# A LoRA linear layer on one core: chunk 2 loaded in 48 and 16 rows, and the drains of three engines put elsewhere or left out

## The chip, the core and the metric

The kernel runs on one core of a Trainium2 chip. The metric is device time in microseconds (us) of one execution, less is better. Before the change the median of 15 runs is 161.18 us (161.04 to 161.37). The profile is of one further execution of 161.05 us.

## The reference

```python
x_flat = x.reshape(-1, in_dim)            # 32768 x 256, float32
y = x_flat @ W                            # W: 256 x 256
lora_out = ((x_flat @ lora_A) * lora_E) @ lora_B    # rank 16
return (y + scale * lora_out).reshape(batch, seq_len, out_dim)   # float32
```

The input x is 33.55 MB and the output as much; the weights are small.

## The kernel before, in words

The low-rank part is folded into one matrix at the start (`weff` = W + A·E·B·scale, L229 to L246 on VectorE and L285 to L291 on TensorE), so that each row of x is multiplied once.

**Chunks, rows and homes.** The 32768 rows are cut into four chunks of 8.39 MB. A chunk lies in SBUF as 128 partitions of 64 rows of 1 KB, so that a partition's part of a chunk is 64 KB, contiguous in HBM. There are three homes for four chunks (`home(c)`, c modulo 3): chunk 3 is loaded into chunk 0's home after chunk 0 has been stored. The result of each row overwrites the row in its home.

**The queue.** One list, ORDER (L18 to L33), gives the order of the transfers that SyncE (SP) issues: ("L", c, s, e) loads rows s to e of each partition of chunk c (L156), and ("S", c, s, e) stores them (L161). A DMA of r rows makes one packet of r KB for each partition, 128 packets in all. A load of chunk 3 waits for the stores of chunk 0 that cover its rows (L155), a store waits for the rows to be computed (L160, `s_done`). All six loads of chunks 0 to 2 are issued at the start, one behind the other. The first store, ("S", 0, 0, 40), is queued behind them.

**The groups.** A chunk is 16 groups of 4 rows. For each of the 64 groups GpSimd (POOL) casts the rows to bfloat16 (`stage`, L200), TensorE transposes them (L258), VectorE copies the transposed words out of PSUM (`xt`, L242), TensorE multiplies by `weff` (L269) and ScalarE (ACT) copies the result home (L221).

**The hold.** At the first group of chunk 2, named HELD (L39), GpSimd waits until the first store has landed (HOLDERS, L40, the wait in `gpsimd_program`), and so do all engines behind it.

**The drains.** `drain(engine, n)` (L170 to L175) waits on its engine for the load that begins at HELD and then issues n drain instructions that do nothing else. It is called at HELD by GpSimd (10), ScalarE (22) and VectorE (12); the counts stand in L44 to L46. The instructions lengthen the engine's program, which is fetched from HBM by DMAs of its own, in packets of 8192 bytes on queue 14.

**The ends of chunk 2.** SP stores rows 2 to 62 of chunk 2. Its first two and last two rows are stored by GpSimd in three DMAs (`share`, L164 to L168) over the partition ranges in SHARES (L37): 108 to 113, 0 to 108, 113 to 128. Each makes packets of 4096 bytes on queue 0.

Of the kernel before, what the change touches and what calls it, by code (L numbers as in the profile page):

```python
# [21 lines left out]
    ("L", 0, 40, 64),  # L22
    ("L", 1, 0, 32),
    ("L", 1, 32, 64),
    ("L", 2, 0, 64),
    ("S", 0, 0, 40),
    ("S", 0, 40, 64),
    ("L", 3, 0, 32),
# [10 lines left out]
HELD = (2, 0)  # L39
# [1 line left out]

WARM_UP = 2

VECTOR_DRAINS = 12  # L44
GPSIMD_DRAINS = 10
SCALAR_DRAINS = 22  # L46

CG = 4
GPC = ROWS // CG
# [8 lines left out]
def kernel(  # L58
# [37 lines left out]
    loaded = {op: sem(f"loaded_{op[1]}_{op[2]}") for op in ORDER if op[0] == "L"}  # L96
# [22 lines left out]
    def home(c):  # L119
        return homes[c % N_HOMES]  # L120

    sync, gpsimd, scalar, vector, tensor = nc.sync, nc.gpsimd, nc.scalar, nc.vector, nc.tensor
# [41 lines left out]
    def share(engine, p, landed):  # L164
        def ends_of(rows):
            return rows[p].rearrange("p (q b) k -> p q b k", b=END_ROWS)[:, :: ROWS // END_ROWS - 1, :, :]

        engine.dma_start(out=ends_of(y_chunks[SHARED]), in_=ends_of(home(SHARED))).then_inc(landed, 16)  # L168

    def drain(engine, n):  # L170
        for op, landed in loaded.items():
            if op[1:3] == HELD:
                engine.wait_ge(landed, 16)
        for _ in range(n):
            engine.drain()  # L175

    def gpsimd_program():
        gpsimd.memset(ident[:], 0.0).then_inc(s_ident, 1)  # L178
        gpsimd.wait_ge(s_ident, 1)
        gpsimd.affine_select(  # L180
            out=ident[:],
            in_=ident[:],
            compare_op=ALU.not_equal,
            fill=1.0,
            base=0,
            pattern=[[-1, P]],
            channel_multiplier=1,
        ).then_inc(s_ident, 1)
        for g in range(N_GROUPS):
            c, b = g // GPC, g % GPC * CG  # L190
            for op, landed in loaded.items():
                if op[1:3] == (c, b):
                    gpsimd.wait_ge(landed, 16)
            if (c, b) == HELD:
                drain(gpsimd, GPSIMD_DRAINS)
                for op in HOLDERS:
                    gpsimd.wait_ge(stored[op], 16)
            if g >= NS:
                gpsimd.wait_ge(s_turned, g - NS + 1)
            gpsimd.tensor_copy(out=stage[g % NS][:], in_=home(c)[:, b:b + CG, :]).then_inc(s_stage[g % UNROLL], 1)  # L200

        gpsimd.wait_ge(s_turned, N_GROUPS - NS + 1)
        gpsimd.drain().then_inc(s_stage[N_GROUPS % UNROLL], 1)
        gpsimd.wait_ge(s_shared, 1)
        for p in SHARES:
            share(gpsimd, p, shared_stored)

    def scalar_program():
        for name, to, of in (
            ("w", w_sb, W.rearrange("(q t) m -> q t m", t=KT)),  # L210
            ("b", b_sb, lora_B),
            ("e", e_sb, lora_E[:, None]),
        ):
            ins = scalar.dma_start(out=to[:], in_=of).then_inc(set_up_loaded[name], 16)
            opening.append(ins.ins.name)
        for g in range(N_GROUPS):
            c, b = g // GPC, g % GPC * CG
            if (c, b) == HELD:
                drain(scalar, SCALAR_DRAINS)
            scalar.wait_ge(s_y, g + 1)  # L220
            scalar.copy(out=home(c)[:, b:b + CG, :], in_=psum_y[g % NY][:]).then_inc(s_free[(g + NY) % UNROLL], 1)  # L221
            if (c, b + CG) == (SHARED, ROWS):
                scalar.drain().then_inc(s_shared, 1)
            if g in ends:
                scalar.drain().then_inc(s_done, 1)  # L225

    def vector_program():
        vector.wait_ge(set_up_loaded["e"], 16)
        vector.wait_ge(s_pe_set_up, 1)  # L229
        vector.tensor_scalar(  # L230
            out=ate[:],
            in0=psum_y[0][:R, :KT, :P],
            scalar1=e_sb[:],
            scalar2=float(scale),
            op0=ALU.mult,
            op1=ALU.mult,
        ).then_inc(s_ate, 1)
        for g in range(N_GROUPS):
            if (g // GPC, g % GPC * CG) == HELD:
                drain(vector, VECTOR_DRAINS)  # L240
            vector.wait_ge(s_turned, g + 1)
            vector.tensor_copy(out=xt[g % NX][:], in_=psum_xt[g % NT][:].bitcast(BF16)).then_inc(s_xt[g % UNROLL], 1)  # L242
            if g == 0:
                vector.wait_ge(set_up_loaded["w"], 16)
                vector.wait_ge(s_pe_set_up, 2)
                vector.tensor_add(out=weff[:], in0=w_sb[:], in1=psum_y[1][:, :KT, :]).then_inc(s_free[0], 1)  # L246
                vector.drain().then_inc(s_free[1], 1)

    def tensor_program():
        def turn(i, result=None):  # L250
# [53 lines left out]
    with tc.tile_critical(no_gpsimd_drain=True):  # L304
        sync_program()
        gpsimd_program()
        scalar_program()
        vector_program()
        tensor_program()
# [35 lines left out]
```

## Time and profile before

| What | Value |
|---|---|
| median of 15 runs | 161.18 us |
| the profiled execution, its own time | 161.05 us |
| its span, first to last instruction | 159.70 us |
| busy: PE, POOL, ACT, DVE | 95.1, 69.3, 66.1, 45.4 us |
| moved by DMA | 67.43 MB, mean 422 GB/s over the span |
| queue 1 (SP's loads and stores) | 2016 packets, 66.60 MB |
| queue 0 (GpSimd's stores) | 224 packets, 0.52 MB |
| queue 14 (instructions), in the span | 3 packets, 0.02 MB |
| loads of chunks 0 to 2 issued | 0.43 to 4.37 us |
| first store issued, landed | 28.68, 74.91 us |
| last store issued | 122.97 us |

The page of the profile gives busy time by engine, the span in 40 slices with the DMA rate in each, the DMA queues, the chain of waits that ended last, and groups of instructions by line. Windows of the span can be asked for: each gives the busy time of the engines, the granted TensorE clock (PEclk), the mean busy share of the 16 DMA engines, and the rate in GB/s; a window counts a packet where it starts.

Beneath these views the trace records every DMA packet with its start, its duration, its queue and its size. The record does not name the DMA engine, but the packets follow each other end to start within a few ns and so join into exactly 16 sequences, called lanes here, one for each DMA engine. In the middle of a run of equal packets a packet of 64 KB takes 2.418 us, one of 40 KB 1.514, of 32 KB 1.213, of 24 KB 0.912, of 16 KB 0.611, and an instruction packet 0.309 us.

### The profile page before, as it was taken

What the parts mean: (1) busy time and instruction counts of PE and PEld (TensorE: products, weight loads), DVE (VectorE), ACT (ScalarE), POOL (GpSimd) and SP (SyncE); (2) the same over time, 40 slices, a digit from 0 to 9 for tenths busy, and PEclk for the clock granted to TensorE, in tenths of its full rate; (3) what the DMA queues carried; (4) which work ended last, traced back from release to release, by engine and by line L of the source; (5) the groups of instructions that cost most, each with busy time, mean ns of one, the idle gap of its engine ahead of it and who ended that gap; (6) DMA issues with size and microseconds to landing.
All of it is one profiled execution on the core that took longest, in us unless ns stands there. A gap on an engine that the chain in (4) does not pass through costs nothing.

```text
span 159.7 us, 2070 instructions
## 1 busy us (share of the span) xinstructions
PE 95.1 (60%) x782; PEld 83.8 (52%) x782; DVE 45.4 (28%) x66; ACT 66.1 (41%) x65; POOL 69.3 (43%) x73
## 2 busy tenths in 40 slices
PE   2669999999999700000999999999995000000000
PEld 1146999999999600000789999999994000000000
DVE  0113555555555400000155555555551000000000
ACT  3001677777777700000257777777776000000000
POOL 1072777777777100002577777777763000000000
PEclk9965999999999995555589999999999655555555
DMA  7999999999979897989999999999989998979986
GB/s 271 427 443 443 400 453 427 484 402 394 591 328 525 361 427 328 466 359 441 412 476 412 419 468 419 533 394 394 509 371 400 482 454 352 529 327 498 425 380 263
DMA packets 2451, 67.43 MB, mean 422 GB/s; under 512 B 512, under 2 KB 528, under 8 KB 784
## 3 DMA queue, kind: packets, MB, share of 16 engines
q1 hardware_dynamic: 2016, 66.60, 97.5%
q0 software_dynamic: 224, 0.52, 0.9%
q10 hardware_dynamic: 208, 0.28, 0.6%
q14 instruction: 3, 0.02, 0.0%
HBM read 33.85 MB, written 33.55 MB: 422 GB/s over the span
## 4 chain that ended last, share of the span: by engine, by line
PE 40%; DMA 34%; POOL 1%; ACT 1%; issue 0%; SPq 0%; ACTq 0%
DMA out_dram<-home 29%; PE psum_y L269 25%; PE psum_xt L258 14%; DMA home<-in_x_dram 5%; POOL stage L200 1%; ACT home L221 1%; PE psum_y L291 1%; SPq L147 0%; ACTq L225 0%
## 5 line engine op out<-in xcount | busy, mean ns | idle before, releaser
L200 POOL CAST stage<-home 128x1024 bf16<-128x1024 f32 x64 | 66.5, 1042 | 48.8 <-DMA out_dram<-home 22.3
L221 ACT COPY home<-psum_y 128x1024 f32<-128x1024 f32 x64 | 64.8, 1013 | 54.8 <-PE psum_y L269 54.8
L269 PE MATMUL psum_y<-weff,xt 128*128 128x256 bf16 x512 | 68.7, 279 | 0.0
L242 DVE COPY xt<-psum_xt 128x1024 bf16<-128x1024 bf16 x64 | 44.3, 692 | 67.0 <-PE psum_xt L258 67.0
L258 PE MATMUL psum_xt<-ident,stage 128*128 128x128 f32 x260 | 41.6, 284 | 23.9 <-POOL stage L200 23.9
L269 PEld LDWEIGHTS psum_y<-weff,xt 128*128 128x128 bf16 x512 | 51.4, 100 | 6.2
L258 PEld LDWEIGHTS psum_xt<-ident,stage 128*128 128x128 f32 x260 | 31.9, 147 | 26.3 <-issue 25.1
L282 PE MATMUL psum_y<-ident 128*128 128x512 f32 x4 | 3.4, 1006 | 2.9 <-POOL ident L180 2.9
L282 PEld LDWEIGHTS psum_y<-ident 128*128 128x128 f32 x4 | 1.2, 323 | 3.9 <-POOL ident L180 2.9
L168 POOL DMA_DIRECT2D out_dram<-home x3 | 2.0, 676 | 1.0 <-PE psum_xt L258 1.0
L230 DVE TENSOR_SCALAR ate<-psum_y,e_sb 16x256 f32<-16x256 f32 x1 | 0.5, 472 | 6.6 <-DMA e_sb<-in_lora_E_dram 6.6
L221 ACT ACT_TABLE_LOAD x1 | 1.3, 1283 | 2.0 <-SPq L304 2.0
L291 PE MATMUL psum_y<-b_sb,ate 16*128 16x256 f32 x4 | 2.1, 670 | 0.0
L291 PEld LDWEIGHTS psum_y<-b_sb,ate 16*128 16x128 f32 x4 | 1.2, 319 | 0.5 <-issue 0.3
L246 DVE TENSOR_TENSOR weff<-w_sb,psum_y 128x512 bf16<-128x512 f32 x1 | 0.7, 687 | 1.4 <-PE psum_y L291 1.4
L178 POOL MEMSET ident<- 128x128 f32 x1 | 0.2, 205 | 1.7 <-SPq L304 1.7
L285 PEld LDWEIGHTS psum_y<-ident,a_sb 128*16 128x16 f32 x2 | 0.2, 114 | 0.9 <-issue 0.9
L180 POOL TENSOR_SCALAR_AFFINE_SELECT ident<-ident 128x128 f32<-128x128 f32 x1 | 0.3, 284 | 0.2 <-POOL ident L178 0.2
L285 PE MATMUL psum_y<-ident,a_sb 128*16 128x128 f32 x2 | 0.4, 273 | 0.0
L326 POOL MEMSET const-float32-0.0<- 128x1 f32 x1 | 0.1, 93 | 0.2 <-issue 0.2
L326 POOL MEMSET const-bfloat16-1.0<- 128x1 bf16 x1 | 0.1, 96 | 0.0
L326 POOL MEMSET const-uint8-127<- 128x1 uint8 x1 | 0.1, 96 | 0.0
(1 smaller groups left out, 0.1 us busy)
## 6 DMA issues: line engine op xcount, KB each, us to landing
home<-in_x_dram SPq DMA_DIRECT2D x4, 4096.0 KB, 24.4
out_dram<-home SPq DMA_DIRECT2D x1, 7680.0 KB, 37.9
home<-in_x_dram SPq DMA_DIRECT2D x2, 3072.0 KB, 16.8
out_dram<-home SPq DMA_DIRECT2D x1, 5120.0 KB, 46.2
out_dram<-home SPq DMA_DIRECT2D x1, 3072.0 KB, 45.7
home<-in_x_dram SPq DMA_DIRECT2D x1, 2048.0 KB, 7.7
out_dram<-home POOLq DMA_DIRECT2D x1, 432.0 KB, 31.5
w_sb<-in_W_dram ACTq DMA_DIRECT2D x1, 256.0 KB, 2.7
```

The costliest lines, as they stand in the source:

```text
L168: engine.dma_start(out=ends_of(y_chunks[SHARED]), in_=ends_of(home(SHARED))).then_inc(landed, 16)
L200: gpsimd.tensor_copy(out=stage[g % NS][:], in_=home(c)[:, b:b + CG, :]).then_inc(s_stage[g % UNROLL], 1)
L221: scalar.copy(out=home(c)[:, b:b + CG, :], in_=psum_y[g % NY][:]).then_inc(s_free[(g + NY) % UNROLL], 1)
L230: vector.tensor_scalar(out=ate[:], in0=psum_y[0][:R, :KT, :P], scalar1=e_sb[:], scalar2=float(scale), op0=ALU.mult, op1=ALU.mult,).then_in ...
L242: vector.tensor_copy(out=xt[g % NX][:], in_=psum_xt[g % NT][:].bitcast(BF16)).then_inc(s_xt[g % UNROLL], 1)
L246: vector.tensor_add(out=weff[:], in0=w_sb[:], in1=psum_y[1][:, :KT, :]).then_inc(s_free[0], 1)
L258: ins = tensor.transpose(psum_xt[i % NT][:, b, :], words[:, b, :], ident[:])
L269: ins = tensor.matmul(psum_y[i % NY][:, b, :], xt[i % NX][:, b, t::KT], weff[:, t, :], start=(t == 0), stop=(t == KT - 1),)
L282: tensor.matmul(psum_y[1][:, :2, :], ident[:], ident[:, None, :].to_broadcast([P, 4, P]), start=True, stop=True)
L285: ins = tensor.transpose(psum_y[0][:R, t, :P], a_sb[:, t, :], ident[:])
L291: ins = tensor.matmul(psum_y[1][:, t, :], ate[:, t, :], b_sb[:], start=True, stop=True)
L326: nc = _bacc.Bacc("TRN2", target_bir_lowering=False, num_devices=1)
```

## The change

The load of chunk 2 is issued as two DMAs, of rows 0 to 48 and of rows 48 to 64. GpSimd's wait for a load at a group's start covers the second piece at group 12 of the chunk, since it looks the pieces up in `loaded`. The function `drain` and its three calls at HELD go. VectorE gets 9 drains after the `weff` add of group 0, GpSimd 7 ahead of its loop, and ScalarE none.

```diff
-    ("L", 2, 0, 64),
+    ("L", 2, 0, 48),
+    ("L", 2, 48, 64),
...
-VECTOR_DRAINS = 12
-GPSIMD_DRAINS = 10
-SCALAR_DRAINS = 22
+VECTOR_DRAINS = 9
+GPSIMD_DRAINS = 7
...
-    def drain(engine, n):
-        for op, landed in loaded.items():
-            if op[1:3] == HELD:
-                engine.wait_ge(landed, 16)
-        for _ in range(n):
-            engine.drain()
-
     def gpsimd_program():
...
         ).then_inc(s_ident, 1)
+        for _ in range(GPSIMD_DRAINS):
+            gpsimd.drain()
         for g in range(N_GROUPS):
...
             if (c, b) == HELD:
-                drain(gpsimd, GPSIMD_DRAINS)
                 for op in HOLDERS:
                     gpsimd.wait_ge(stored[op], 16)
...
-            if (c, b) == HELD:
-                drain(scalar, SCALAR_DRAINS)
             scalar.wait_ge(s_y, g + 1)
...
-            if (g // GPC, g % GPC * CG) == HELD:
-                drain(vector, VECTOR_DRAINS)
             vector.wait_ge(s_turned, g + 1)
...
                 vector.drain().then_inc(s_free[1], 1)
+                for _ in range(VECTOR_DRAINS):
+                    vector.drain()
```

## The prediction

> **What bounds the kernel now.** I read the page's slices first, then the chain of waits, then windows of the span, then the packet records.
>
> The slices show the DMA engines full from the second slice to the last, while PE stands still for five slices in the middle and for the last nine: only the DMA has no slack.
>
> ```profile
> PE   2669999999999700000999999999995000000000
> DMA  7999999999979897989999999999989998979986
> HBM read 33.85 MB, written 33.55 MB: 422 GB/s over the span
> ```
>
> The chain of waits names TensorE for 40% of the span, and this misleads. Its pieces in order of time end with ScalarE's copy at 121.90, after which the last store is issued (122.97) and lands 36.7 us later. The store's own 8.39 MB take 19.3 us at the 434 GB/s of a full window, so it stood 17 us behind older packets. Compute may end up to 17 us later at no cost. The chain also holds the 46.23 us between the first store's issue and its landing, of which 32.7 us (28.68 to 61.36) are loads queued ahead.
>
> ```profile
> 28.68 46.23 DMA out_dram<-home
> 74.91 0.05 issue
> 74.96 1.05 POOL stage L200
> ```
>
> So the end is set by the lane (DMA engine) that finishes last: bytes at full rate, plus whatever time a lane loses. The next view looks for lost time. These windows are cut where whole rounds of 16 packets start, one per lane; the last number of a row is GB/s, the second is the length.
>
> ```profile
> 53.27:55.69 2.42, 1.81 (x17) 1.42 (x14) 1.05 (x2) 1.83 (x3) 0.00 (x0) 1.00 1.00 433
> 55.70:58.12 2.42, 0.00 (x0) 0.00 (x0) 0.00 (x0) 0.43 (x1) 0.00 (x0) 1.00 1.00 433
> 58.12:61.35 3.23, 0.00 (x0) 0.00 (x0) 0.00 (x0) 0.00 (x0) 0.00 (x0) 0.85 1.02 325
> 61.35:62.87 1.52, 0.00 (x0) 0.00 (x0) 0.00 (x0) 0.00 (x0) 0.00 (x0) 0.50 1.00 431
> 62.87:64.38 1.51, 0.00 (x0) 0.00 (x0) 0.00 (x0) 0.00 (x0) 0.00 (x0) 0.50 1.00 434
> ```
>
> The third row is chunk 2's last round of 64 KB packets, right ahead of the first store: 3.23 us in place of 2.42, at the full busy share. The store's 40 KB packets behind it run at full rate at once. By the packet records all 16 packets of that round are long, by 0.59 to 1.04 us, mean 0.87. There is one more place where loads give way to a store: chunk 3's 32 KB packets ahead of chunk 1's store.
>
> ```profile
> 97.66:98.87 1.21, 1.21 (x13) 1.13 (x12) 0.59 (x2) 0.91 (x2) 1.01 (x2) 1.00 1.00 433
> 98.87:100.08 1.22, 1.22 (x14) 1.12 (x12) 0.60 (x2) 0.92 (x2) 0.96 (x1) 1.00 1.07 432
> 100.08:102.50 2.42, 2.42 (x25) 2.26 (x23) 1.36 (x2) 1.82 (x3) 2.08 (x2) 1.00 1.01 434
> ```
>
> Here almost nothing is lost: the last packets of the 16 lanes are long by 0 to 0.46 us, mean 0.09. One turn from loads to stores costs 0.87 us a lane with 64 KB packets ahead, the other 0.09 with 32 KB ahead. That is the profile's case for the split.
>
> **The split, step by step.** All lanes lose at the first turn, so what counts is each lane's end less its own loss. From the records: the latest lane ends at 159.37 and lost 0.99, which leaves 158.38; the others near it are 159.19 less 0.82, 158.37; 159.15 less 0.86, 158.28; 159.14 less 0.89, 158.25; 158.91 less 0.67, 158.24. With no loss at all the end would be 158.38, 0.99 earlier.
>
> What the loss is with 16 KB packets, no row shows. It is bounded below by nothing (no packet in the trace is shorter than the usual one of its size by more than 3 ns, so a turn gives nothing back), above by the 0.87 mean that 64 KB packets show. I take 0.09, the row of 32 KB, since 32 KB is the nearest size; a loss in proportion to size from 64 KB would be 0.22.
>
> The smaller packets cost a little by themselves. Eight of 64 KB a lane take 8 x 2.418 = 19.34 us. A 48 KB packet, read off between 40 KB (1.514) and 60 KB (2.267), is 1.815, so the new eight pairs take 8 x (1.815 + 0.611) = 19.41, less 0.02 since packets overlap by 3 ns. With the 4-byte packet that closes the second DMA that is +0.05 us.
>
> Sum: end at 158.38 + 0.09 + 0.05 = 158.52 against 159.37, **0.85 us earlier**.
>
> The second issue takes SP some 0.45 us at 4.4 us; SP then waits until 28.68 for the first store, so nothing is behind it. GpSimd's added wait at group 12 of chunk 2 is for a load that landed by 62.3, some 30 us before; a wait instruction and its dispatch is 0.1 us, inside the 17 us.
>
> The Trainium skill ("DMA: Bandwidth & Descriptors", Anatomy of one DMA) speaks against more DMAs: its fit gives each a fixed cost of about 2.0 us, measured on GpSimd's path. By it the sum would be 2.0 - 0.85, 1.15 us slower. This trace has it otherwise for queued transfers: the window 97.66 to 98.87, inside a row of loads issued one behind the other, runs at 433 GB/s.
>
> **The drains, step by step.** In engine time they are nothing. VectorE's twelve ran from 62.35 to 62.80, GpSimd's ten from 62.40 to 63.00, both inside the hold, and ScalarE's 22 from 80.10 to 81.28, where the copy after them began 1.33 us late; all that is in the 17 us. Nine on VectorE after the `weff` add are 9 x 0.04 = 0.36 us, against 0.57 us idle ahead of the copy at 13.77; seven on GpSimd are 7 x 0.06 = 0.43 us, in the 5.3 us idle ahead of the first cast. Even uncovered, what they delay is the first store's issue, 32.7 us ahead of its turn.
>
> What the drains move is fetches, which cost lanes. Three instruction packets lie in the span, at 67.52, 67.61 and 85.84, each some 4.7 us after a run of drains. Each takes 0.31 us of its lane, and the packet behind it is long by 0.35, 0.47 (40 KB stores) and 0.25 us (a 32 KB load): 0.66, 0.78 and 0.56 us in all. They fall on three lanes, which by the records carry 1 or 2 of queue 0's 4096-byte packets where most carry 10: 8 x 0.159 = 1.27 us less, which is their cover. I expect three fetches again, on the same lanes. ScalarE's moves most: the instruction in the place of its last drain is now 22 further on, which is the copy at 106.2, so the packet lands near 111 among chunk 1's 64 KB stores. VectorE's and GpSimd's land between 48 and 60 or between 80 and 88, by which of the drains called them.
>
> What a fetch makes its lane lose among 64 KB stores, no row shows. Bounds for the long packet: nothing, and 1.04, the longest stretch of any packet; I take 0.47, the nearest store row. ScalarE's lane then ends at 159.05 - 0.99 + 0.14 - 0.56 + 0.31 + 0.47 = 158.42, before the 158.52 above: hidden. At 1.04 it ends at 158.99 and eats 0.47 of the gain. The lane that ended at 158.91 stands at 158.24 + 0.14 - 0.66 + 0.31 = 158.03 plus its long packet, hidden up to 0.49; the third fetch lane has over 1 us.
>
> The profiled execution took 161.05, of which 1.35 lie outside the span: 161.05 - 0.85 = 160.20. The median shown is 0.13 above it, so **160.3** is the forecast.
>
> **The rivals.**
> 1. **The loss belongs to the first store, not to packet size.** The two turns differ in more than the load's packets: one is the first write of the run with compute standing still, the store behind it has 40 KB packets, the other's 64 KB. If the stretch is a price of that first turn, it lands on the last 16 KB packets instead. Against it: the store's own packets show no delay, the load's do. Then only +0.05 is left: 161.2, no change.
> 2. **Slower: a fetch among 64 KB stores.** If the first turn keeps its loss and ScalarE's fetch stretches its neighbour by 1.04, its lane ends at 159.05 - 0.56 + 0.31 + 1.04 + 0.05 = 159.89, 0.52 after the present end: 161.7. It decides on the end from a long packet of 0.52 on, and passes 0.2% (0.32 us, about what a measurement of this kernel can tell) from 0.84 on. Both must hold: without the loss the same lane is 0.38 earlier than today's end.
>
> **How the numbers follow.** Forecast 0.66 (two turns, one pointing each way in size, is thin evidence; the mechanism of the loss is not shown), first rival 0.20, second 0.14. The forecast's own range is 160.05 (all of the 0.99 gone, less the 0.14 between median and fastest run) to 160.8 (the dear fetch, or a loss in proportion plus noise). To keep 8 in 10 it reaches over the first rival: 161.2 plus the 0.19 from median to slowest run, 161.4. Faster by over 0.2% 0.66, within 0.2% 0.20, slower 0.14.
>
> **What would show it.** The last round of loads ahead of the first store near 0.61 us a packet, and the window from there to the first 40 KB packets at about 430 GB/s. The first store landing near 74.1 in place of 74.91, and all of the second half as much earlier. Three packets on queue 14, one near 111. The lanes ending at about 158.5. If the 16 KB packets are stretched by 0.87 in sum, the first rival is right; if a fetch lane ends last, the second's mechanism acts. The forecast falls also if the loss spreads over several rounds, since all eight rounds of 16 KB lie within 5 us of the turn.

## The result, and the profile after

The changed kernel takes **161.72 us** (median of 9 runs, 161.66 to 162.08) against 161.12 before (46 runs); the ratio is 1.0040, 95% interval 1.0032 to 1.0048. It is slower, by 0.6 us, and outside the range that was given; measured again later, on one chip with other versions, it came out at 1.0020 (`after_again` below). The profiled execution took 161.99 us, its span 160.7.

What the prediction looked for first is the turn from loads to the first store, at about 61 us. (The second turn is the one from chunk 3's loads to chunk 1's store, at about 100 us. What a lane loses is the time that its packets take over the usual, and the time that it stands idle.) The windows are cut as before, at rounds of packets (length, then busy time by engine, PEclk, DMA share, GB/s):

```profile
55.68:58.11 2.43, 0.00 (x0) 0.00 (x0) 0.00 (x0) 0.15 (x1) 0.00 (x0) 1.00 1.01 421
58.11:61.43 3.32, 0.00 (x0) 0.00 (x0) 0.00 (x0) 0.00 (x0) 0.00 (x0) 0.60 1.00 316
61.43:62.94 1.51, 0.00 (x0) 0.00 (x0) 0.00 (x0) 0.00 (x0) 0.00 (x0) 0.50 1.00 429
62.94:64.45 1.51, 0.00 (x0) 0.00 (x0) 0.00 (x0) 0.00 (x0) 0.00 (x0) 0.50 1.00 434
```

The second row is the last rounds of loads, now of 16 KB: 316 GB/s where 64 KB packets gave 325. The loss is all there. By the packet records it now lies on two to four of each lane's last 16 KB packets, which take up to 1.36 us in place of 0.61; 15 of the lanes lose 0.91 us each on the mean, against 0.87 for all 16 before.

The first store lands 0.8 us later, not earlier, as SP's timeline shows (start, how long the group lasted, what): its load of chunk 3 waits for that landing, 75.73 against 74.92 before. It lands when the last lane has carried its part: the last 40 KB packet ends at 75.38, before at 74.44, and it is on the lane that the table below follows.

```profile
27.18 9.40 SPq L161 DMA_DIRECT2D out_dram<-home  x2
75.73 7.68 SPq L156 DMA_DIRECT2D home<-in_x_dram  x2
83.46 41.18 SPq L161 DMA_DIRECT2D out_dram<-home  x3
```

And at the end one lane is alone. In the last stretch the kernel before starts no packet:

```profile
157.00:159.00 2.00, 0.00 (x0) 0.00 (x0) 0.00 (x0) 0.00 (x0) 0.00 (x0) 0.50 0.00 0
```

the changed kernel starts one, 64 KB in 2 us:

```profile
157.00:159.00 2.00, 0.00 (x0) 0.00 (x0) 0.00 (x0) 0.00 (x0) 0.00 (x0) 0.50 0.08 33
```

The records say which lane that is. Fifteen lanes end between 158.2 and 159.17, this one at 160.30. Followed back, it is the lane of the instruction packet at 55.98:

| Where, on that lane | Lost, us |
|---|---|
| instruction packet at 55.98, and the 16 KB packet behind it (1.265) | 0.33 + 0.65 |
| first turn: idle 60.01 to 60.70, a packet of 1.00, idle 61.71 to 61.94, a packet of 0.74 | 0.69 + 0.39 + 0.23 + 0.13 |
| second turn, at 99.59: a 32 KB packet of 2.36 | 1.15 |
| sum | 3.57 |

The other lanes lose 0.91 at the first turn, and the lane carries 8 packets of queue 0 less (1.27 us). By this sum it is 3.57 - 0.91 - 1.27 = 1.39 us behind the rest; its end lies 1.5 us behind the mean of the other fifteen, 158.78. The other two instruction packets, at 80.16 and 107.48, made the packets behind them long by 0.10 and 0.17 us and cost nothing at the end.

### The profile page after: what moved, and what is told of

Same layout as the page of the kernel before. It is cut to its first block, busy times and chain, and to the rows that moved or that the text cites. A ratio compares the mean times of both kernels' runs of the same rounds, so it can differ in the third digit from the quotient of the medians.

```text
span 160.7 us, 2043 instructions
## 1 busy us (share of the span) xinstructions
PE 94.8 (59%) x782; PEld 83.3 (52%) x782; DVE 45.4 (28%) x66; ACT 66.1 (41%) x65; POOL 68.9 (43%) x73
## 4 chain that ended last, share of the span: by engine, by line
PE 39%; DMA 35%; POOL 1%; ACT 1%; DVE 0%; issue 0%; SPq 0%; ACTq 0%; POOLq 0%; DVEq 0%
DMA out_dram<-home 30%; PE psum_y L261 25%; PE psum_xt L250 13%; DMA home<-in_x_dram 5%; POOL stage L194 1%; ACT home L213 1%; PE psum_y L283 1%; DVE weff L236 0%; SPq L147 0%; ACTq L217 0%; POOLq L193 0%; DVEq L235 0%
## 5 line engine op out<-in xcount | busy, mean ns | idle before, releaser
L283 PE MATMUL psum_y<-b_sb,ate 16*128 16x256 f32 x4 | 1.1, 400 | 0.0
L283 PEld LDWEIGHTS psum_y<-b_sb,ate 16*128 16x128 f32 x4 | 0.7, 184 | 0.2 <-issue 0.2
```

Source lines behind the costliest of these rows:

```text
L283: ins = tensor.matmul(psum_y[1][:, t, :], ate[:, t, :], b_sb[:], start=True, stop=True)
```

## The experiments

All ratios are to the kernel before, run beside them. Two theories were set against each other at first. **F**: the slow-down is the fetch that VectorE's nine early drains bring to 56 us, shortly before the turn; the turn's loss does not depend on packet size. **S**: the split itself slows the lanes. A third, **A**, blamed ScalarE's fetch at 107.5.

### One part of the change at a time

The split alone, with the drains of before waiting for both pieces of chunk 2:

```diff
-    ("L", 2, 0, 64),
+    ("L", 2, 0, 48),
+    ("L", 2, 48, 64),
...
-            if op[1:3] == HELD:
+            if op[1] == HELD[0]:
                 engine.wait_ge(landed, 16)
```

> The kernel before with chunk 2 loaded in 48 and 16 rows, and its drains at the hold as before (they wait for both pieces, so that they run at about 62 us). Theory F (the slow-down is an instruction fetch that lands shortly before the turn from loads to stores and makes its lane late; the loss of about 0.9 us a lane at the turn does not depend on the packets' size): 161.1 to 161.2, like before, the turn's loss spread over several 16 KB packets, all lanes ending within 1 us. Rival S (the split itself slows the lanes): 161.6 to 161.8, one lane over 1 us late with no fetch in it.

Measured: 161.27 us, ratio 1.0005 (0.9996 to 1.0015). Loss at the turn 0.80 us a lane, spread over 43 long packets of 16 KB. Its window of that stretch:

```profile
58.05:61.22 3.17, 0.00 (x0) 0.00 (x0) 0.00 (x0) 0.00 (x0) 0.00 (x0) 0.59 1.04 336
```

So the split neither helps nor harms, as far as this interval can tell. The fixed 2.0 us a DMA of the Trainium skill's fit ("DMA: Bandwidth & Descriptors", Anatomy of one DMA), which was made for DMAs that GpSimd issues, does not show on SP's queue: one more DMA in it costs under 0.25 us, the upper end of that interval.

The drains alone, chunk 2 whole:

```diff
 (of the changed kernel)
-    ("L", 2, 0, 48),
-    ("L", 2, 48, 64),
+    ("L", 2, 0, 64),
```

> The changed kernel with chunk 2 loaded whole: the drains moved, nothing else. Theory F: a fetch again lands between 56 and 61 us, now between 64 KB packets; its lane is late at the turn and ends last: 161.4 to 161.9. Rival S (the split is to blame): 161.1.

Measured: 161.30 us, 1.0009 (0.9996 to 1.0022). The packet comes at 55.81, its lane turns late (the last 64 KB load is long by 1.69 us, the others' by 0.92 on the mean), loses 0.68 more at the second turn and ends last, at 159.85 against 159.09. That is theory F in the lanes, but less time than the 0.4% of the whole change. The time itself lies between the two theories, and its interval holds 1. Whether the split adds to a late lane's loss was tried by running both again on one chip:

> The changed kernel once more, beside the next on the same chip: 161.6 to 161.8, ratio 1.003 to 1.005.

> The changed kernel with chunk 2 loaded whole once more, beside the one above. If the slow-down is the fetch alone: the same time as the one above within 0.1%. If the split adds to it (a late lane loses more with 16 KB packets left than with 64 KB ones): 161.1 to 161.4, at least 0.15% less than the one above.

Measured: 161.54 us, 1.0020 (1.0004 to 1.0037), and 161.49, 1.0016 (1.0002 to 1.0030). The expected ratio of the first was missed, and the two are alike. The moved drains carry the slow-down, and no share of the split in it can be told. Executions of these two spread from 160.8 to 162.26, while those of kernels without a late lane lie mostly within 0.5 us: how much the late lane loses differs from one execution to the next. In the profiled execution of after_again, of 161.15 us, it lost 0.67 at the second turn in place of 1.15 and ended at 159.46.

### Whose fetch it is

VectorE without drains, the rest as changed:

```diff
-VECTOR_DRAINS = 9
+VECTOR_DRAINS = 0
```

> The changed kernel with no drains on VectorE, so that the fetch called by VectorE comes nine instructions later in its stream, after the hold. Theory F with VectorE as the one that calls the packet at 56.0: that packet moves to 80 to 90 us, no lane is late at the turn, 161.1 to 161.2. If GpSimd calls it: the packet stays at 56 and the time at 161.7. Rivals S and A (the fetch of ScalarE among 64 KB stores): 161.7.

Measured: **160.96 us, 0.9988** (0.9980 to 0.9997). The packet at 56 is gone, there is one at 89.5 instead. The slow-down is undone, and a little more. (The profiled execution of it took 161.57, 0.6 above its median. In it the lanes lose some 0.7 us each at the second turn too, which no other profile shows; why is not known.)

ScalarE's 22 drains put back at the hold, the rest as changed:

```diff
+SCALAR_DRAINS = 22
...
+            if (c, b) == HELD:
+                for op, landed in loaded.items():
+                    if op[1] == HELD[0]:
+                        scalar.wait_ge(landed, 16)
+                for _ in range(SCALAR_DRAINS):
+                    scalar.drain()
             scalar.wait_ge(s_y, g + 1)
```

> The changed kernel with the 22 drains of ScalarE put back at the hold, so that its fetch comes near 86 us and not at 107.5. Rival A (that fetch costs the time): 161.1. Theory F: no change, 161.7, the packet at 56.0 still there and its lane last.

Measured: 161.59 us, 1.0026 (1.0012 to 1.0041). ScalarE's packet moved to 85.96, the one at 55.87 stayed, its lane ends last, at 159.87, and the time stayed, within the intervals. Theory A falls.

### Near the turn, or just late at it

```diff
-VECTOR_DRAINS = 9
+VECTOR_DRAINS = 20
```

> The changed kernel with 20 drains on VectorE in place of 9, so that its fetch is called 11 copies (of 1.31 us each) earlier and lands near 41.6 us, among 48 KB loads and 20 us ahead of the turn. Theory N (what costs is nearness to the turn): the lane loses about 0.6 to 1.0 us at the fetch and no more than the others at the turn, its cover of 1.27 us holds: 161.0 to 161.3. Rival L (what costs is that the lane is late when the others turn, whenever it became late): it again loses 1.3 to 1.8 us at the first turn and up to 1 us at the second, and ends last: 161.5 to 161.9.

Measured: 161.77 us, 1.0034 (1.0020 to 1.0049). The packet lands at 43.25, 18 us before the turn; with the 48 KB packet behind it (long by 0.66) the lane falls 0.99 us behind. At the turn it loses 1.77 us (two packets long by 1.16 and 0.56, and 0.05 of idle time and smaller excesses) where the others lose some 0.9, at the second 0.50, and it ends last, at 160.10 against 159.11. **Rival L holds: a lane that comes late to the turn loses more there, whether it became late at 43 or at 56 us.** Nor is one of the 16 lanes slow at the turn in itself: in the kernel before, where the fetches come after it, none loses more than 1.04 us there. In the last stretch one packet starts, as in the changed kernel:

```profile
157.00:159.00 2.00, 0.00 (x0) 0.00 (x0) 0.00 (x0) 0.00 (x0) 0.00 (x0) 0.50 0.08 33
```

### Is the split worth anything once the fetch is away

The changed kernel with chunk 2 whole and VECTOR_DRAINS = 0:

> The changed kernel with chunk 2 loaded whole and no drains on VectorE: against the same with 48 and 16 rows (ratio 0.9988) only the split differs. Theory F with a loss at the turn that does not depend on packet size: the same ratio, 0.998 to 1.000. If the split is worth something by itself: slower than that by more than 0.1%, 161.15 or more.

Measured: **160.97 us, 0.9987** (0.9977 to 0.9997), the same as with 48 and 16 rows, and lanes that end between 158.11 and 159.22. The gain on the kernel before is small, but the intervals of both end below 1; it is thus from the drains: the fetches now come at 78.4, 90.7 and 107.4. These two versions beat both kernels, by 0.1% over before.

### What the loss at the turn is

In the kernel before, four rows of chunk 0 are stored ahead of chunk 2's load:

```diff
+    ("S", 0, 0, 4),
     ("L", 2, 0, 64),
-    ("S", 0, 0, 40),
+    ("S", 0, 4, 40),
...
-HOLDERS = (("S", 0, 0, 40),)
+HOLDERS = (("S", 0, 4, 40),)
```

> The kernel before with the first 4 rows of chunk 0 stored ahead of chunk 2's load, so that the first writes of the run come at about 42 us, behind 32 KB loads, and the turn at 61 us is no longer the first. Theory P (the loss is a price of the run's first store): 0.5 us or more a lane at 42, under 0.2 at 61. Theory Q (the loss belongs to what the turn at 61 is like, not to being first): 0.7 to 1.1 a lane at 61 as before. Time 160.9 to 161.7 either way, since a second turn is added.

Measured: 161.11 us, 0.9999 (0.9989 to 1.0009). The loss has moved. The windows are the rounds ahead of the small store, the small store, and the last 64 KB round ahead of the big one:

```profile
39.00:42.08 3.08, 3.08 (x31) 2.89 (x29) 1.58 (x3) 2.19 (x4) 2.54 (x3) 1.00 0.79 255
42.08:43.34 1.26, 1.26 (x14) 1.17 (x13) 0.69 (x1) 0.96 (x2) 0.72 (x2) 1.00 1.09 449
57.80:60.20 2.40, 0.00 (x0) 0.00 (x0) 0.00 (x0) 0.00 (x0) 0.00 (x0) 0.50 1.01 437
60.23:62.64 2.41, 0.00 (x0) 0.00 (x0) 0.00 (x0) 0.00 (x0) 0.00 (x0) 0.50 0.94 408
```

The packet records are finer than windows that cut through spread lanes: 0.80 us a lane are lost between 39 and 42, behind 32 KB loads and with all engines at work; at 61, behind 64 KB packets, no packet of the 16 is over its 2.418 us by more than 0.04. Theory P holds: **the price belongs to the first store of the run**, not to packet size, and not to the turn as such. (The one profile that does not fit is that of `after_no_vector_drains`, which pays some 0.7 us at the second turn as well.) The time does not gain by it, since the price is only paid earlier.

Compute at work through the turn (the changed kernel with HOLDERS empty and no drains):

> The changed kernel without its drains and without the hold, so that chunk 2 is computed as soon as its first piece is there and all engines work through the turn at 61 us. Theory C (the loss is there because compute stands still at the first turn and not at the second): the loss at 61 falls to 0.2 us a lane or less, 160.2 to 160.7. If it stays at 0.7 to 1.1, compute has nothing to do with it: 161.0 to 161.3.

Measured: 161.88 us, 1.0041 (1.0027 to 1.0055), 1.07 us a lane lost at 61, though TensorE is busy for all of the 3.00 us from 60 to 63. Theory C falls. The time is above what either theory expected, and why was not followed up: one lane ends at 160.08, the next at 159.55. No fetch comes before the turn here (they lie at 70.9, 75.7 and 102.9), so a time like the changed kernel's can also come about in another way.

Can the price be paid early by other transfers? Both are on the version with chunk 2 whole and no drains on VectorE:

```diff
+                if c == 3:
+                    sync.wait_ge(first_written, 16)
...
+        ins = scalar.dma_start(out=y_chunks[3, :, 0:1, :], in_=x_chunks[3, :, 0:1, :]).then_inc(first_written, 16)
+        opening.append(ins.ins.name)
...
```

> Chunk 2 whole and no drains on VectorE (0.9987 of before), with one transfer more: the first DMA of ScalarE's queue copies 1 KB for each of 128 partitions from the input to the output in HBM, over rows that the last store writes later. So the run's first writes to HBM come at about 1 to 2 us, when the lanes are not yet full. Theory W (the loss is a price of the first writes to HBM, and can be paid while the lanes have nothing to do): under 0.2 us a lane at 61, 160.2 to 160.7. Theory X (the price is of the first read of SBUF by the DMA): 0.7 to 1.1 at 61 as before, 160.9 to 161.1.

```diff
+        sync.wait_ge(first_read, 16)
...
+        scalar.wait_ge(s_ident, 2)
+        scalar.dma_start(out=copy_sb[:], in_=ident[:]).then_inc(first_read, 16)
```

> Chunk 2 whole and no drains on VectorE, with one transfer more: at about 3 us ScalarE's queue copies 512 bytes for each of 128 partitions from SBUF to SBUF. No early write to HBM. Theory X (the price is of the first read of SBUF by a DMA): the loss moves to 3 to 5 us and is under 0.2 us a lane at 61; time 160.3 to 161.1 by how much of it the first loads hide. Theory W (first write to HBM): 0.7 to 1.1 a lane at 61, 160.9 to 161.1.

Measured: 161.58 us, 1.0027 (1.0015 to 1.0039), and 161.19, 0.9993 (0.9980 to 1.0005). The loss at 61 stays, 0.74 and 0.95 us a lane. Both theories fall in this form: neither an HBM to HBM copy nor an SBUF to SBUF copy on ScalarE's queue takes the price away. The first takes 0.6 us more than the kernel that it is made from; its lanes start the first store that much later already (62.14 to 62.59 against 61.30 to 61.92), with the copy ahead of x's first packets.

How much must be stored? One row of chunk 0 (8 KB a lane) ahead of chunk 2's load, and 4 KB of one partition:

```diff
+    ("S", 0, 0, 1),
     ("L", 2, 0, 64),
-    ("S", 0, 0, 40),
+    ("S", 0, 1, 40),
...
-HOLDERS = (("S", 0, 0, 40),)
+HOLDERS = (("S", 0, 1, 40),)
```

> The kernel before with only the first row of chunk 0 (8 packets of 1 KB a lane, 8 KB) stored ahead of chunk 2's load. Theory B (the loss is the time to bring some 23 KB a lane of store data in ahead, 0.87 us at 27.1 GB/s, once): with 8 KB only some 0.3 us a lane is lost at 42 and the rest, 0.5 to 0.6, at 61. Theory O (the first store of the run on that queue costs its price whatever its size): 0.7 or more at 42, under 0.1 at 61. Time 161.0 to 161.3.

```diff
+    ("E",),
     ("L", 2, 0, 64),
...
+            if op[0] == "E":
+                sync.wait_ge(s_first, 1)
+                sync.dma_start(out=y_chunks[0, 0:1, 0:4, :], in_=home(0)[0:1, 0:4, :]).then_inc(one_stored, 16)
+                continue
...
```

> The kernel before with 4 rows of one partition (4 KB in all) stored ahead of chunk 2's load, so that one lane, or a few if the DMA is spread, turns at 42. If the price belongs to each lane: 15 lanes lose 0.6 to 1.0 us at 61 as before, and the one that turned early loses nothing there. If it belongs to the core's memory or path as a whole: all lanes are under 0.2 us at 61. Time 161.0 to 161.3 in the first case, 160.3 to 160.7 in the second.

Measured: 161.16 us, 0.9997 (0.9987 to 1.0006), with 0.07 us a lane lost at 39 and 1.18 at 61; and 161.15, 1.0004 (0.9991 to 1.0016), with nothing at 41 and 0.66 at 61. Neither theory B nor O fits the first: 8 KB a lane pay almost nothing and spare nothing later. The second: a store of one partition spares none of the 16 lanes, not even the one that carried it (the shortest of the 16 long packets is over by 0.25 us; the lane that carried it, followed from its packet at 41.35, lost 0.78). What remains: 32 KB a lane, stored on all lanes in packets of 4 KB, pay the price in full; 8 KB a lane in packets of 1 KB do not. What lies between was not tried, nor whether the packets' size or the sum decides.

## Why the prediction was wrong, point by point

- **What bounds the kernel: right.** The lane that ends last sets the time, and compute's slack was never touched.
- **The split's gain: the step that failed first.** "I take 0.09, the row of 32 KB, since 32 KB is the nearest size": measured 0.80 (split_only) and 0.91. Two turns that differed in size also differed in being first, and I read the difference as one of size. On this step the first rival, at 0.20, was the right one; early_store shows it, with a loss of 0.80 behind 32 KB packets and none behind 64 KB.
- **The packets' own cost, +0.05: not contradicted**; split_only's +0.0005 with its interval cannot tell 0.05 us.
- **The drains cost no engine time, three fetches on the three lanes with little of queue 0: right.** VectorE's packet came at 55.98, inside the 48 to 60 given, GpSimd's at 80.16, ScalarE's at 107.48 for the 111 estimated.
- **The fetch's price: the step that made it slower.** I priced a fetch by its own 0.31 us and the one long packet behind it, "hidden up to 0.49". Measured at 55.98: 0.65 for that packet, already over that 0.49, and then two terms that the sum did not have: 0.53 us more than the other lanes at the first turn (1.44 less 0.91) and 1.15 at the second, for being late. The cover of 1.27 us, enough after the first store, was not enough before it.
- **The second rival** named 161.7 and the time is 161.72, but by another engine: its fetch was ScalarE's at 107, which cost 0.17 beyond its own packet. That its number comes out is luck. What it had right is that the first turn keeps its loss and a fetch lane ends last.

The Trainium skill ("Runtime: NRT & Kernel Launch", Instruction fetch mechanics) says of a fetch that its cost is mostly hidden, and for the engine the trace agrees where it can tell: ScalarE's copies go on every 1.31 us (106.20, 107.51, 108.82) past its packet at 107.48. VectorE's packet at 55.98 cannot show it, since its last copy ahead of the hold began at 53.94. For the transfers beside it the trace differs: VectorE's fetch set its lane back by 0.98 us.

**Left open**: what the first store's price is made of, why 8 KB a lane neither pay nor spare it, why the kernel without the hold is as slow as the changed one, and how a lane that is late loses more at a turn (it idles for 0.92 us there in the changed kernel, which the records show but do not explain).

## What to carry to other kernels

Where all DMA engines are full to the end, follow each lane through the packet records, and price an event by what its lane loses up to the end of the run, not by the packet behind it. Move what makes one lane late, such as an instruction fetch, behind the places where all lanes change direction together, or give that lane less to carry. Before a loss is put down to a size, look for what else differs between the places that show it and those that do not: here one was simply the first.

## What the runs showed of the hardware that was not expected

- The first sizable store of a run costs each lane 0.66 to 1.18 us on the mean, on the loads ahead of it, in every kernel tried, with loads of 16, 32 or 64 KB; the second turn costs under 0.15 on the mean (in all profiles but that of `after_no_vector_drains`, some 0.7). An earlier store of 32 KB a lane takes the price with it (0.80 at 39 to 42 us, then nothing at 61).
- An 8 KB instruction packet makes the packet behind it 0.65 to 0.66 us longer when it falls among loads before the first store (at 43.25 and, in five profiles, at 55.81 to 55.98), and 0.09 to 0.63 after it (at 67 to 108). All the early ones are VectorE's, and VectorE's at 89.5 to 91.3 still cost 0.55 to 0.63, where GpSimd's at 78 to 81 cost 0.09 to 0.22 and ScalarE's at 105 to 108 cost 0.11 to 0.18: whether the place or the engine decides was not told apart.
- A lane that comes some 1 us late to the first turn loses 1.2 to 1.77 us there (0.8 to 1.1 for the others). It comes 1.2 to 1.8 us behind the median lane to the second and loses 0.50 to 1.15 there (under 0.1 on the mean for the others), so that 1 us grows to over 2. In the other profiles the lanes that came 0.6 to 0.8 us late to the second turn lost 0.02 to 0.52 there. That is less on the whole, and fits that a fetch between the turns was cheap.
